# Order of the four token sums within each weight pass of the token-major projections

## The chip, the cores and the metric

The kernel runs on one core of a Trainium2 chip. The metric is device time in microseconds (us), the median over runs of one program. TensorE is called PE below, its weight loads PEld, VectorE DVE, ScalarE ACT, GpSimd POOL, and the queue that issues most transfers SP.

## What is computed

One layer of a diffusion backbone over 512 latent and 256 context tokens of width 1024, in float32. A combined projection of the modulated input feeds three branches (a gated linear recurrence, differential attention, a chunked spatial gate); each is gated, projected, scaled by a sigmoid gate and summed, and one output projection follows. What matters here is three of the products:

```
px = split_proj(modulate(x, sh_x, sc_x), w_in, b_in)      # px[6], px[7]: 512 tokens x 1024
sgu_x = spatial_gating(px[6], px[7], ln_g, ln_b, w_s, b_s)
...
return (s_a * y_a + s_b * y_b + s_c * y_c) @ w_out        # 512 tokens x 1024
```

`px[7]`, `px[6]` and the first 512 columns of the product with `w_out` are the three token-major projections of this document: the result has tokens on the partitions.

## The kernel before, in words

Every float32 operand is held as a high and a low part, and a product is three matmuls: high by high, high by low, low by high (`mm3`, lines 62 to 64). Most projections are channel-major: one weight tile of 128 columns, one PSUM sum of 512 tokens, 24 matmuls of 512 columns.

The token-major ones work on 512 output columns at a time. There are four sums, one for each block `tt` of 128 tokens; each is 128 x 512 float32. The four lie in two PSUM tiles of 128 x 1024 (`bk`, from the pool `big` of three): sums 0 and 1 share the first tile, 2 and 3 the second. A weight request of 512 rows (one half of the contraction) makes one pass: `proj_th` issues 12 matmuls for each `tt`, so a pass has 48. Two passes (`half` 0 and 1) complete the four sums. After the 12 matmuls of `half` 1 of a `tt`, DVE reads that sum out of PSUM: at line 1066 it adds the bias (`proj_tokens`, used for `vz`, sums named `sv`, and for `u`), at line 1225 it multiplies by the gate row (`residual`, sums named `out`), followed there by two more DVE operations (lines 1226 and 1228). `proj_tokens` does this for two column halves `j`, the output projection once. So five passes have readouts: those of the weights w61 and w63 (`sv`), w81 and w83 (`u`) and w109 (`out`). The passes of w60, w62, w80, w82 and w108 have none.

PE's instructions run in the order in which the program writes them. The other engines' order is made by the framework's scheduler. The framework keeps one record for each tile: a PE write to a tile waits for a readout of that tile that stands before it in the program, whichever columns either of them touches.

Weights come through three `raw` buffers of 512 KB (SP, lines 105 to 113), are cast on ACT (line 133) and their low part is formed on DVE or POOL (line 134). `pump` starts one such piece after each group of matmuls, once the weights that held the slot are used up.

```
for half in range(2):
    W = w_next()
    for tt in range(4):
        ps = bk[tt // 2][:, tt % 2 * 512:tt % 2 * 512 + 512]
        proj_th(ps, X, tt, W, half)
        pump()
        if half == 1:
            done = V.tensor_tensor(dst[:, tt, cs], ps, bias[:, cs], ALU.add)
```

Of the kernel before, what the change touches and what calls it, by code (L numbers as in the profile page):

```python
# [29 lines left out]
def block_kernel(ctx, tc, x, c, cctx_in, c_ctx, w_ada, b_ada, w_in, b_in, conv_w, conv_b,  # L30
# [19 lines left out]
    def big_t(name):  # L50
        return big.tile([P, 1024], F32, tag="big", name=name)
# [18 lines left out]
    def proj_th(ps, X, tt, W, half):  # L70
        mm3(ps, X, W, [np.s_[:, 4 * half + k, tt * P:(tt + 1) * P] for k in range(4)],
            [np.s_[:, k, :] for k in range(4)], half == 0, half == 1)
# [66 lines left out]
    def pump(n=1):  # L139
        for _ in range(n):  # L140
            if state["conv"] >= len(pieces):
                return
            i, part = pieces[state["conv"]]
            if part == 0 and not all(retired(x) for x in reqs[i][4]):
                return
            w_conv()

    def w_next():
        i = state["use"]
        state["use"] += 1  # L150
        while state["conv"] < len(pieces) and pieces[state["conv"]][0] <= i:
            w_conv()
        return parts[i]
# [900 lines left out]
    def proj_tokens(dst, bias, name, then=None):  # L1054

        for j in range(2):
            cs = slice(j * 512, j * 512 + 512)
            bk = [big_t(f"{name}{j}_{t}") for t in range(2)]
            for half in range(2):
                W = w_next()  # L1060
                for tt in range(4):
                    ps = bk[tt // 2][:, tt % 2 * 512:tt % 2 * 512 + 512]
                    proj_th(ps, X, tt, W, half)
                    pump()
                    if half == 1:
                        done = V.tensor_tensor(dst[:, tt, cs], ps, bias[:, cs], ALU.add)
                if then is not None:
                    then(2 * j + half, done if half else None)

    vz = sp.tile([P, 4, D], F32, name="vz")  # L1070
    def hs_a(step, done):
# [6 lines left out]
        with tc.issue_after(done.ins):  # L1078
            for g in range(8):
                V.tensor_tensor(hsA[:, 1, g, :], pa[:, g, :], f(hsA[:, 0, g, :]), ALU.subtract)  # L1080

    proj_tokens(vz, bvv, "sv", hs_a)
    lg = bcast(sgu_ln_g[0], "lg")
    lb = bcast(sgu_ln_b[0], "lb")
# [47 lines left out]

    u = gp.tile([P, 4, D], F32, tag="c", name="u")
    proj_tokens(u, bcast(b_in[0, 6 * D:7 * D], "bu"), "u")

    def sgu_mm(g):
# [85 lines left out]
    def residual(tt, c0, n, ps, j):  # L1222
        cs = slice(c0, c0 + n)
        tm = op.tile([P, 512], F32, tag="tm", bufs=2, name=f"tm{tt}_{j}")
        V.tensor_tensor(tm[:, 0:n], ps, gt[:, cs], ALU.mult)
        V.scalar_tensor_tensor(xr[:, tt, cs], xr[:, tt, cs], ALPHA, tm[:, 0:n], op0=ALU.mult,
                               op1=ALU.add)
        V.bn_stats(sto[:, tt, j, :], xr[:, tt, cs])
# [7 lines left out]
    bk = [big_t(f"out{t}") for t in range(2)]  # L1236
    for half in range(2):
        W = w_next()
        for tt in range(4):
            ps = bk[tt // 2][:, tt % 2 * 512:tt % 2 * 512 + 512]  # L1240
            proj_th(ps, M, tt, W, half)
            pump()
            if half == 1:
                residual(tt, 0, 512, ps, 0)
# [71 lines left out]
```

## Time and profile before

| what | value |
|---|---|
| median of 3 runs | 1033.73 us (1033.44 to 1035.08) |
| the profiled execution | 1034.09 us, of which its span is 1032.1 us |
| PE busy | 968.8 us (94%), 5239 matmuls |
| DVE busy | 659.7 us (64%) |
| ACT busy | 525.3 us (51%) |
| POOL busy | 155.0 us (15%) |
| mean granted clock of TensorE | 0.978 |
| transfers | 103.34 MB, mean 100 GB/s |

The span runs from the first to the last instruction. Busy time of PE is modelled: matmuls overlap, each lasting longer than the distance to the next. So the pace of PE is read from the starts of matmuls, not from their durations. A figure in brackets behind a row of a timeline is how long the engine was idle before it, and what ended the idle time.

### The profile page before, as it was taken

What the parts mean: (1) busy time and instruction counts of PE and PEld (TensorE: products, weight loads), DVE (VectorE), ACT (ScalarE), POOL (GpSimd) and SP (SyncE); (2) the same over time, 40 slices, a digit from 0 to 9 for tenths busy, and PEclk for the clock granted to TensorE, in tenths of its full rate; (3) what the DMA queues carried; (4) which work ended last, traced back from release to release, by engine and by line L of the source; (5) the groups of instructions that cost most, each with busy time, mean ns of one, the idle gap of its engine ahead of it and who ended that gap; (6) DMA issues with size and microseconds to landing.
All of it is one profiled execution on the core that took longest, in us unless ns stands there. A gap on an engine that the chain in (4) does not pass through costs nothing.

```text
span 1032.1 us, 13231 instructions
## 1 busy us (share of the span) xinstructions
PE 968.8 (94%) x5239; PEld 815.7 (79%) x5239; DVE 659.7 (64%) x996; ACT 525.3 (51%) x741; POOL 155.0 (15%) x118
## 2 busy tenths in 40 slices
PE   5997799989989998999999999899999999999996
PEld 4796688878878887778888887778887778888876
DVE  4479788788787663787777775368333256325557
ACT  3155846646647796897777795223221134323221
POOL 1143424333242252100000000000000000000002
PEclk8999999989989999899999999999999999999999
DMA  9933220130130131213332223625223322754212
GB/s 312 289 102 83 62 62 21 43 102 22 42 103 21 41 103 45 68 51 103 102 92 82 82 87 97 235 82 162 82 82 109 95 71 76 252 172 145 97 48 82
DMA packets 142996, 103.34 MB, mean 100 GB/s; under 512 B 3629, under 2 KB 133142, under 8 KB 142934
## 3 DMA queue, kind: packets, MB, share of 16 engines
q1 hardware_dynamic: 140790, 95.85, 30.4%
q0 software_dynamic: 2000, 6.56, 2.4%
q8 instruction: 41, 0.67, 0.3%
q14 instruction: 21, 0.17, 0.0%
q10 hardware_dynamic: 144, 0.10, 0.0%
HBM read 94.10 MB, written 4.19 MB: 95 GB/s over the span
## 4 chain that ended last, share of the span: by engine, by line
PE 64%; DVE 17%; ACT 11%; DMA 4%; issue 3%; SPq 1%; POOL 0%; POOLq 0%; ACTq 0%; DVEq 0%
PE y L62 4%; PE gt L62 4%; PE gt L64 4%; PE gt L63 4%; PE y L64 4%; PE y L63 4%; DVE mxn L732 2%; DVE e L747 2%; DVE kd L582 2%; ACT rt L859 1%; DVE kd L587 1%; PE s L722 1%; PE gc L62 1%; PE gc L64 1%; PE out L62 1%
## 5 line engine op out<-in xcount | busy, mean ns | idle before, releaser
L133 ACT CAST w<-raw 128x1024 fp32r<-128x1024 f32 x96 | 99.8, 1045 | 85.3 <-PE y L64 23.8
L134 DVE TENSOR_TENSOR w<-raw,w 128x1024 fp32r<-128x1024 f32 x71 | 86.6, 1224 | 77.5 <-ACT w L133 77.4
L62 PE MATMUL gt<-xhl,w 128*128 128x512 f32 x192 | 75.6, 394 | 1.3 <-ACT pad L882 1.3
L64 PE MATMUL gt<-xhl,w 128*128 128x512 f32 x192 | 74.8, 390 | 0.0
L63 PE MATMUL gt<-xhl,w 128*128 128x512 f32 x192 | 74.8, 390 | 0.0
L722 PE MATMUL s<-kd,qdq 128*128 128x512 f32 (+1 forms) x256 | 58.6, 368 | 17.2 <-ACT e L737 6.2
L134 POOL TENSOR_TENSOR w<-raw,w 128x1024 fp32r<-128x1024 f32 x25 | 61.0, 2444 | 67.5 <-ACT w L133 67.5
L722 PEld LDWEIGHTS s<-kd,qdq 128*128 128x128 f32 x256 | 44.4, 195 | 29.0 <-issue 15.0
L732 DVE TENSOR_REDUCE mxn<-s 128x1 f32<-128x768 f32 x64 | 58.3, 949 | 7.5 <-PE s L722 7.5
L737 ACT ACTIVATE e<-s,mxn 128x768 f32<-128x768 f32 x32 | 28.8, 899 | 51.1 <-DVE mxn L732 51.0
L1197 POOL PARTITION_BROADCAST grb<-grs x8 | 3.8, 581 | 308.3 <-DVE grs L1194 308.3
L62 PEld LDWEIGHTS gt<-xhl,w 128*128 128x128 f32 x192 | 36.1, 188 | 9.1 <-ACT pad L882 1.5
L64 PEld LDWEIGHTS gt<-xhl,w 128*128 128x128 f32 x192 | 36.0, 188 | 7.7
L63 PEld LDWEIGHTS gt<-xhl,w 128*128 128x128 f32 x192 | 36.1, 188 | 7.1
L964 POOL DMA_DIRECT2D pa_d<-ha x8 | 4.4, 551 | 227.4 <-DVE ha L963 227.4
L747 DVE SCALAR_TENSOR_TENSOR e<-s,sm,e 128x768 f32<-128x768 f32 x32 | 32.6, 1017 | 6.5 <-ACT e L740 5.7
L54 ACT CAST vh<-v 128x128 fp32r<-128x128 f32 x48 | 12.4, 263 | 43.0 <-PE v L64 19.7
L859 ACT ACT_TABLE_LOAD x25 | 32.1, 1283 | 0.4
L62 PE MATMUL xa<-xhl,w 128*128 128x512 f32 x64 | 26.3, 411 | 4.8 <-ACT pad L882 4.8
L765 DVE TENSOR_TENSOR wtl<-t,wth 128x768 fp32r<-128x768 f32 x32 | 30.3, 950 | 0.6 <-ACT wth L763 0.5
L740 ACT ACTIVATE e<-e,sm 128x768 f32<-128x768 f32 x32 | 29.9, 935 | 0.2 <-DVE sm L739 0.2
L859 ACT ACTIVATE rt<-ri,colB 128x770 f32<-128x770 f32 x32 | 27.6, 905 | 2.5 <-PE ri L64 1.8
(458 smaller groups left out, 3043.7 us busy)
## 6 DMA issues: line engine op xcount, KB each, us to landing
raw<-in_w_in_dram SPq DMA_DIRECT2D x96, 512.0 KB, 3.8
raw<-in_w_branch_dram SPq DMA_DIRECT2D x24, 512.0 KB, 3.9
ada<-in_w_ada_dram SPq DMA_DIRECT2D x6, 1024.0 KB, 8.4
qdq<-qdq POOLq DMA_DIRECT2D x16, 256.0 KB, 3.0
adg<-in_w_ada_dram SPq DMA_DIRECT2D x8, 512.0 KB, 6.0
raw<-in_w_out_dram SPq DMA_DIRECT2D x8, 512.0 KB, 3.8
xtok<-in_x_dram SPq DMA_DIRECT2D x4, 512.0 KB, 5.5
ada<-in_w_ada_dram SPq DMA_DIRECT2D x4, 512.0 KB, 6.0
```

What stands on the lines that cost most here:

```text
L62: PE.matmul(ps, ah, bh, start=(first and i == 0), stop=False)
L63: PE.matmul(ps, ah, bl, start=False, stop=False)
L64: PE.matmul(ps, al, bh, start=False, stop=(last and i == n - 1))
L133: state["hi"] = S.copy(h, raws[j])
L134: state["lo"].tensor_tensor(l, raws[j], f(h), ALU.subtract)
L722: PE.matmul(sp[:, sl], qds[h][:, 2 * m + j, qs], kds[h][:, m, sl], start=(j == 0), stop=(j == 1))
L732: V.tensor_reduce(mxn[:, m:m + 1], sps[m][:, 0:TA], mybir.AxisListType.X, ALU.max, negate=True)
L737: S.activation(e, sps[m][:, 0:TA], AF.Exp, bias=mxn[:, m:m + 1], accum_out=sm[:, m:m + 1])
L740: S.mul(es[i][0], es[i][0], sm[:, 0:1])
L747: V.scalar_tensor_tensor(e0, e1, sm[:, 1:2], e0, op0=ALU.mult, op1=ALU.add)
L765: V.tensor_tensor(wts[h][1][:, :, qs], src, f(wts[h][0][:, :, qs]), ALU.subtract)
L859: order[0] = S.activation(out, in_, fn, **kw)
```

## The change

In both places the loop over the four sums runs in the order 0, 2, 1, 3, for `half` 0 and `half` 1 alike.

```
@@ proj_tokens
             for half in range(2):
                 W = w_next()
-                for tt in range(4):
+                for tt in (0, 2, 1, 3):
                     ps = bk[tt // 2][:, tt % 2 * 512:tt % 2 * 512 + 512]
                     proj_th(ps, X, tt, W, half)
                     pump()
@@ the first 512 columns of the output projection
     for half in range(2):
         W = w_next()
-        for tt in range(4):
+        for tt in (0, 2, 1, 3):
             ps = bk[tt // 2][:, tt % 2 * 512:tt % 2 * 512 + 512]
             proj_th(ps, M, tt, W, half)
             pump()
```

First place, PE in the pass of w61: the three rows on either side of the border between the first and the second group of 12 matmuls, before. `sv_0` is the first PSUM tile (sums 0 and 1), `sv_1` the second; `waits DVE_49` is a wait for DVE's counter.

```order
L62 MATMUL sv_0_5596<-w61h,xhl 128x512
L63 MATMUL sv_0_5596<-w61l,xhl 128x512
L64 MATMUL sv_0_5596<-w61h,xhl 128x512
L62 MATMUL sv_0_5596<-w61h,xhl 128x512 [waits DVE_49]
L63 MATMUL sv_0_5596<-w61l,xhl 128x512
L64 MATMUL sv_0_5596<-w61h,xhl 128x512
```

The same engine and pass with the change, at the borders from the first group to the second and from the second to the third:

```order
L62 MATMUL sv_0_5596<-w61h,xhl 128x512
L63 MATMUL sv_0_5596<-w61l,xhl 128x512
L64 MATMUL sv_0_5596<-w61h,xhl 128x512
L62 MATMUL sv_1_5597<-w61h,xhl 128x512
L63 MATMUL sv_1_5597<-w61l,xhl 128x512
L64 MATMUL sv_1_5597<-w61h,xhl 128x512
...
L62 MATMUL sv_0_5596<-w61h,xhl 128x512 [waits DVE_49]
L63 MATMUL sv_0_5596<-w61l,xhl 128x512
L64 MATMUL sv_0_5596<-w61h,xhl 128x512
```

The second group now writes the other tile and has no wait; the wait on the first readout stands one group later, at the third. The wait at the fourth group, on the readout of the tile's first sum, stays at the fourth, but that sum is now the second group's and no longer the third's.

Second place, DVE in the same pass, from the low part of the next weights to the first row that follows the four readouts, before:

```order
L134 TENSOR_TENSOR w62l<-raw_0_5606,w62h 128x1024 [waits DMAHW4_49,Activation_49]
L134 TENSOR_TENSOR w62l<-raw_1_5624,w62h 128x1024 [waits DMAHW5_49,Activation_49]
L1066 TENSOR_TENSOR vz<-sv_0_5596,bvv 128x512 [waits DMAHW7_49,PE_49]
L1092 BN_STATS st_5874<-vz 128x6 [waits DVE_49]
L1066 TENSOR_TENSOR vz<-sv_0_5596,bvv 128x512 [waits PE_49]
L1092 BN_STATS st_5878<-vz 128x6 [waits DVE_49]
L1066 TENSOR_TENSOR vz<-sv_1_5597,bvv 128x512 [waits PE_49] x2
L1080 TENSOR_TENSOR hsA<-pa,hsA 128x512 [waits DMAHW0_49,Activation_49]
```

and with the change:

```order
L134 TENSOR_TENSOR w62l<-raw_0_5606,w62h 128x1024 [waits DMAHW4_49,Activation_49]
L134 TENSOR_TENSOR w62l<-raw_1_5624,w62h 128x1024 [waits DMAHW5_49,Activation_49]
L1066 TENSOR_TENSOR vz<-sv_0_5596,bvv 128x512 [waits DMAHW7_49,PE_49]
L1092 BN_STATS st_5874<-vz 128x6 [waits DVE_49]
L1066 TENSOR_TENSOR vz<-sv_1_5597,bvv 128x512 [waits PE_49]
L1066 TENSOR_TENSOR vz<-sv_0_5596,bvv 128x512 [waits PE_49]
L1092 BN_STATS st_5878<-vz 128x6 [waits DVE_49]
L1066 TENSOR_TENSOR vz<-sv_1_5597,bvv 128x512 [waits PE_49]
L1080 TENSOR_TENSOR hsA<-pa,hsA 128x512 [waits DMAHW0_49,Activation_49]
```

The readouts follow the new order of the sums; what stands ahead of the first readout (the next weights' low part) and behind the last has not moved. ACT, POOL and SP have the same rows in the same order as before.

## Rows read from the trace of the kernel before

**Rows 1.** The page, part 1: busy time, share of the span, instructions.

```profile
PE 968.8 (94%) x5239; PEld 815.7 (79%) x5239; DVE 659.7 (64%) x996; ACT 525.3 (51%) x741; POOL 155.0 (15%) x118
```

**Rows 2.** Waits of PE from 640 us to the end: total us, times, longest.

```profile
PE sv L62 <- DVE vz L1066: 4.2, 4, 1.5
PE u L62 <- DVE u L1066: 4.2, 4, 1.5
PE out L62 <- DVE tm L1225: 2.2, 2, 1.5
```

**Rows 3.** Timeline, pass of w61: start us, us, engine, line, operation.

```profile
656.47 0.39 PE L62 MATMUL sv<-w61h,xhl 128*128 128x512 f32 x1
...
660.08 0.68 DVE L1066 TENSOR_TENSOR vz<-sv,bvv 128x512 f32<-128x512 f32 x1
...
660.82 0.50 PE L62 MATMUL sv<-w61h,xhl 128*128 128x512 f32 x1 [1.47 <-DVE vz L1066]
...
663.88 0.69 DVE L1066 TENSOR_TENSOR vz<-sv,bvv 128x512 f32<-128x512 f32 x1 [2.38 <-PE sv L64]
...
666.17 0.39 PE L64 MATMUL sv<-w61h,xhl 128*128 128x512 f32 x1
...
667.35 0.50 PE L62 MATMUL sv<-w61h,xhl 128*128 128x512 f32 x1 [0.79 <-DVE vz L1066]
...
670.24 0.39 PE L62 MATMUL sv<-w62h,xhl 128*128 128x512 f32 x1
```

**Rows 4.** Timeline of PE: the first matmul of the other passes, or behind them.

```profile
681.12 0.39 PE L62 MATMUL sv<-w63h,xhl 128*128 128x512 f32 x1
...
694.63 0.39 PE L62 MATMUL gt<-xhl,w 128*128 128x512 f32 x1
...
793.75 0.39 PE L62 MATMUL u<-w81h,xhl 128*128 128x512 f32 x1
...
807.51 0.39 PE L62 MATMUL u<-w82h,xhl 128*128 128x512 f32 x1
...
818.39 0.39 PE L62 MATMUL u<-w83h,xhl 128*128 128x512 f32 x1
...
831.85 0.39 PE L62 MATMUL sgu<-vnh,wsh 128*128 128x512 f32 x1
...
986.89 0.39 PE L62 MATMUL out<-w109h,mhl 128*128 128x512 f32 x1
...
1000.63 0.28 PE L62 MATMUL out<-w110h,mhl 128*128 128x256 f32 x1
```

**Rows 5.** Timeline of DVE: first readouts of the other four passes, and w63's low part.

```profile
675.87 2.35 DVE L134 TENSOR_TENSOR w63l<-raw,w63h 128x1024 fp32r<-128x1024 f32 x2
...
684.46 0.68 DVE L1066 TENSOR_TENSOR vz<-sv,bvv 128x512 f32<-128x512 f32 x1
...
797.35 0.68 DVE L1066 TENSOR_TENSOR u<-u,bu 128x512 f32<-128x512 f32 x1
...
821.73 0.68 DVE L1066 TENSOR_TENSOR u<-u,bu 128x512 f32<-128x512 f32 x1
...
990.50 0.69 DVE L1225 TENSOR_TENSOR tm<-out,gt 128x512 f32<-128x512 f32 x1
```

**Rows 6.** Weight pieces (tile raw), 640 to 720 us: issue to landing.

```profile
DMA to landing us min/median/max: 3.4/4.2/5.0
```

**Rows 7.** Windows: stretch, length, busy us of each engine, granted clock (PEclk), DMA.

```profile
219.00:222.00 3.00, 3.00 (x16) 3.00 (x16) 3.00 (x5) 2.73 (x5) 2.64 (x2) 0.50 0.00 0
...
656.40:670.20 13.80, 11.55 (x50) 8.89 (x49) 5.74 (x7) 6.16 (x10) 0.06 (x1) 1.00 0.65 214
```

**Rows 8.** Timeline of PE where the granted clock is 0.50.

```profile
216.74 1.62 PE L722 MATMUL s<-kd,qdq 128*128 128x512 f32 x4 [1.87 <-DVE e L747]
...
218.15 0.41 PE L62 MATMUL v<-w15h,xhl 128*128 128x256 f32 x1
...
221.78 0.41 PE L64 MATMUL v<-w15h,xhl 128*128 128x256 f32 x1
```

More of the change, by code (lines that the diff above doesn't have):

```diff
@@ L1060, in proj_tokens @@
                 W = w_next()
-                for tt in range(4):
+                for tt in (0, 2, 1, 3):
                     ps = bk[tt // 2][:, tt % 2 * 512:tt % 2 * 512 + 512]
@@ L1238, in block_kernel @@
         W = w_next()
-        for tt in range(4):
+        for tt in (0, 2, 1, 3):
             ps = bk[tt // 2][:, tt % 2 * 512:tt % 2 * 512 + 512]
```

## The prediction

> **What bounds the kernel now.** I read the shares of the engines first: PE is busy 94% of the span, the next engine 64% [rows 1]. So the time is PE's own work plus its gaps, and a change that adds no matmul can only act through gaps. The list of PE's waits, from 640 us to the end, comes next: apart from one wait for a weight in the pass of w60, the only waits there are ten, always of a first matmul (line 62) for a readout by DVE: four in `sv`, four in `u`, two in `out` [rows 2]. The channel-major projections between them, some 230 us, show none. The timeline of one pass with readouts then shows how such a wait comes about [rows 3]. The first group of 12 matmuls runs from 656.47; at the pace found below its last starts at 656.47 + 11 x 0.2267 = 658.96, and the next matmul, which belongs to sum 1 in the same tile, starts only at 660.82, right behind the readout of sum 0 (660.08 to 660.76). The third group, in the other tile, starts without a wait while sum 1 is read out (663.88). Then sum 3 waits for the readout of sum 2: 666.17 to 667.35. The reader is to see that each tile costs one wait, and that a readout under matmuls of the other tile holds nobody up: it lasts 0.69 us there, against 0.68 us with PE idle.
>
> **The change part by part.**
>
> *The pace without a wait.* The pass of w62, with no readouts, starts at 670.24 [rows 3] and ends at 681.12 [rows 4]: 10.88 us for 48 matmuls, 0.2267 us each. The pass of w82, 807.51 to 818.39, takes 10.88 us too [rows 4]. Each changes the sum three times and the tile once within those 10.88 us, so changing the target costs nothing that these rows show.
>
> *What a pass with readouts loses now.* Its length less 10.88 us: w61, 656.47 to 670.24, 13.77 us, so 2.89 [rows 3]; w63, 681.12 to 694.63, 13.51, so 2.63; w81, 793.75 to 807.51, 13.76, so 2.88; w83, 818.39 to 831.85, 13.46, so 2.58; w109, 986.89 to 1000.63, 13.74, so 2.86 [rows 4]. The sum is **13.84 us**. In w61 the waits themselves, from start to start less one step, are 1.86 - 0.23 = 1.63 us and 1.18 - 0.23 = 0.95 us [rows 3]; the other 0.3 us of a pass are the slower starts just behind a wait (a matmul of 0.50 us instead of 0.39). I take the length of the passes, since it holds both.
>
> *What the moved waits cost.* With the change the third group waits for the first readout. It is due at pass start + 24 x 0.2267 = 5.44 us. In the pass of w61 that is 661.91; the readout, which stands behind the low part of w62 on DVE and so does not begin when the first group ends, finished at 660.76 [rows 3]: 1.15 us to spare. In the others, with the ends of the first readouts [rows 5] against pass start + 5.44 [rows 4]: w63, 685.14 against 686.56, 1.42 to spare; w81, 798.03 against 799.19, 1.16; w83, 822.41 against 823.83, 1.42; w109, 991.19 against 992.33, 1.14. What comes ahead of these readouts hangs on the end of the pass before, so it keeps its distance from the pass. The fourth group waits for the readout of sum 2. That sum's last matmul ends about 5.6 us into the pass; The first readout ends 4.0 to 4.3 us into the pass by the figures above; what DVE has behind it is at most two operations on 512 columns (`out`) or some statistics (`sv`, lines 1092 and 1093), so it is free by about 6 us, the readout takes 0.7, and the group is due at 8.16 us: over a microsecond to spare. So the ten waits go to zero. Nothing in these rows prices a satisfied wait at a group's start on PE. From below it is nothing: each of the passes without readouts begins with a matmul that waits for a cast long done, and 0.2267 us is kept. From above it is what a matmul behind a wait loses, 0.50 - 0.39 = 0.11 us, ten times 1.1 us. I take nothing, since the nearer rows are those of the passes without readouts, and keep 1.1 us for the range.
>
> *What is hidden.* DVE's four readouts of a pass are the same instructions in another order; they lie under PE. With the third group's sum read later than before, the next tile taken from the pool follows a readout that ends about 9 us into the pass, and its first write comes in the second group of the next pass, at 10.88 + 2.72 = 13.60 us: some 4.6 us to spare. In the output projection two more operations on the same 512 columns follow each readout; counted as long as it (0.69 us [rows 5]), they make 2.1 us for a group of 12 x 0.2267 = 2.72 us of PE, and fit.
>
> *What follows earlier.* Casts and low parts of the next weights start when a pass ends, so they move up with PE. The shortest distance I find is w63's low part: done at 675.87 + 2.35 = 678.22 [rows 5], first used at about 681.35, 3.1 us later; both ends move up by w61's 2.89. Only transfers keep their own length, 3.4 to 5.0 us from issue to landing [rows 6], issued a pass or more ahead. The tail behind PE's last matmul does not change.
>
> *The sum.* The profiled execution took 1034.09 us; less 13.84 is 1020.25. The median of the runs lies 0.36 us below the profiled one, so the forecast for a median is 1033.73 - 13.84 = **1019.9 us**.
>
> *Rule against row.* The rows say that a group which goes on in the same 1024-wide tile waits 1.63 and 0.95 us [rows 3]. The Trainium skill (Perfetto Trace Analysis, Matmuls) says that independent groups should rotate through PSUM banks so that the readout of one overlaps the matmuls of the next, and (PSUM — Partial Sum Buffer, Terms and Specifications) that a bank holds 512 float32 values of a partition. By that rule alone the kernel before rotates already, one bank for each sum, the readouts are covered, and the change gains 0: 1033.7. The rows disagree with this reading: what counts in this program is the tile, and the tile holds two banks.
>
> **The rivals.**
>
> *A readout comes late.* If DVE reaches a first readout more than some 1.2 us later than now (it has a low part ahead of it, 2.35 us long where w63's stands [rows 5]), the third group waits. At worst the five first waits come back in full: 1.63 us in w61, w81 and w109, and 0.26 less in w63 and w83, whose passes lose that much less: 3 x 1.63 + 2 x 1.37 = 7.6 us, and the time is about 1027.5. Against it: the low part hangs on a cast that starts at a fixed point of the pass. For it: the reserve is smallest, 1.14 us, in three of the five.
>
> *The gain is given back behind.* PE gets 13.84 us ahead of the transfers. If a weight piece now lands late by its spread of 5.0 - 3.4 = 1.6 us [rows 6] at two points, some 3.2 us come back: about 1023. Against it: PE waits for no weight behind 656 us today.
>
> *It does nothing.* The wait could follow the second group wherever it is, if the record were coarser than a tile: 1033.7. Against it: sum 2 starts without a wait while sum 1 is read [rows 3]. By the Trainium skill's rule above the result would be the same.
>
> *Slower: the granted clock.* With PE at 0.50 (its 1.2 GHz level) 18 matmuls of 256 columns start 0.2135 us apart (218.15 to 221.78, 17 steps [rows 7, 8]), so 512 columns would take 0.427, 0.20 more than now; a pass would take 9.6 us longer. If the new rhythm of tiles lowered the clock in two passes, they would cost 19.2 us against the 13.84 gained: about 1039. It decides from 13.84 / 0.20 = 69 matmuls on, a pass and a half. Against it: the clock is 1.00 in a pass with both waits in it [rows 7], PE gets busier, and where the clock is 0.50, PE came out of a wait of 1.87 us for the softmax [rows 8], longer than any that this change leaves. The Trainium skill (TensorE: Matmul & The Clock Gate, A second HAM failure mode: psum-queue depth-cycling) tells of a kernel whose cycling through PSUM banks made PE idle briefly between groups, so that the clock swung; by that rule the alternation would cost. The trace has three changes of sum in each pass at 1.00, so it does not bear this out here.
>
> **How the numbers follow.** Forecast 0.87; late readouts 0.05; given back behind 0.04; nothing 0.03; slower clock 0.01. A measurement can tell about 0.2%, 2 us, from no change. The forecast and the first two rivals are faster by far more: 0.96. Nothing is the 0.03 of same, the clock the 0.01 of slower. The range: the runs lie from 0.3 us below to 1.35 us above their median, so the forecast alone gives 1019.6 to 1021.3; 1.1 us for satisfied waits makes that 1022.4; up to about 1023.4 it takes in the weights' late landing. Below I add 1 us, since the runs spread over 1.64 us and three others can have their median elsewhere in that. So 1018.6 to 1023.4.
>
> **What would show it.** Right: the passes of w61, w63, w81, w83 and w109 last about 10.9 us each; the ten waits are gone from PE's list and nothing takes their place; DVE's readouts last 0.7 us still; the clock stays 1.00. Wrong: a wait of a third group for line 1066 or 1225 (late readouts), a wait for line 133 or 134 behind 656 us (given back), or matmuls of 512 columns 0.43 us apart (the clock).

## The result

| | median us | lowest to highest | runs |
|---|---|---|---|
| before | 1034.24 | 1033.44 to 1035.08 | 4 |
| with the change | 1019.13 | 1019.10 to 1021.12 | 4 |

The ratio is 0.9859, with a 95% interval of 0.9842 to 0.9876. The forecast, 1019.9 against 1033.73, was a ratio of 0.9866.

The page of the changed kernel, its span and part 1 (it answers to [rows 1]):

```profile
span 1017.1 us, 13232 instructions
...
PE 965.0 (95%) x5239; PEld 816.1 (80%) x5239; DVE 659.4 (65%) x996; ACT 525.5 (52%) x741; POOL 154.9 (15%) x118
```

The same 5239 matmuls, in a span that is 15.0 us shorter. The list of what PE waited for from 640 us to the end (it answers to [rows 2]; the columns are total us, times, longest):

```profile
PE sv L63 <- DVE w60l L134: 1.1, 1, 1.1
```

The ten waits for readouts are gone and none has come in their place. The one that is left, for the low part of w60, was there before. The timeline of the pass of w61 (it answers to [rows 3]):

```profile
655.39 0.39 PE L62 MATMUL sv<-w61h,xhl 128*128 128x512 f32 x1
...
656.72 2.36 DVE L134 TENSOR_TENSOR w62l<-raw,w62h 128x1024 fp32r<-128x1024 f32 x2 [10.23 <-ACT w62h L133]
...
657.89 0.39 PE L64 MATMUL sv<-w61h,xhl 128*128 128x512 f32 x1
...
658.11 0.39 PE L62 MATMUL sv<-w61h,xhl 128*128 128x512 f32 x1
...
659.00 0.69 DVE L1066 TENSOR_TENSOR vz<-sv,bvv 128x512 f32<-128x512 f32 x1
...
660.83 0.39 PE L62 MATMUL sv<-w61h,xhl 128*128 128x512 f32 x1
...
661.03 0.69 DVE L1066 TENSOR_TENSOR vz<-sv,bvv 128x512 f32<-128x512 f32 x1 [0.62 <-PE sv L64]
...
663.55 0.39 PE L62 MATMUL sv<-w61h,xhl 128*128 128x512 f32 x1
...
666.27 0.39 PE L62 MATMUL sv<-w62h,xhl 128*128 128x512 f32 x1
```

The second group starts 0.22 us after the last matmul of the first, while sum 0 has not been read out yet: DVE is at the low part of w62 until 659.08. The third group, which needs that readout, is due at 660.83; the readout ended at 659.69. The fourth, at 663.55, needs the readout that ended at 661.72. The pass takes 666.27 - 655.39 = 10.88 us.

The other passes with readouts, by the first matmul of each and the one that follows it (they answer to [rows 4]):

```profile
677.15 0.39 PE L62 MATMUL sv<-w63h,xhl 128*128 128x512 f32 x1
...
688.03 0.39 PE L62 MATMUL gt<-xhl,w 128*128 128x512 f32 x1
...
787.17 0.39 PE L62 MATMUL u<-w81h,xhl 128*128 128x512 f32 x1
...
798.05 0.39 PE L62 MATMUL u<-w82h,xhl 128*128 128x512 f32 x1
...
808.93 0.39 PE L62 MATMUL u<-w83h,xhl 128*128 128x512 f32 x1
...
819.81 0.39 PE L62 MATMUL sgu<-vnh,wsh 128*128 128x512 f32 x1
...
974.82 0.39 PE L62 MATMUL out<-w109h,mhl 128*128 128x512 f32 x1
...
985.70 0.28 PE L62 MATMUL out<-w110h,mhl 128*128 128x256 f32 x1
```

All four take 10.88 us, like that of w61, and to the hundredth what a pass without readouts takes. Two of them as windows of the profile (length, busy us of each engine, then the granted clock):

```profile
655.40:666.30 10.90, 10.90 (x50) 9.03 (x49) 5.74 (x7) 6.16 (x10) 0.00 (x0) 1.00 0.84 273
...
974.80:985.70 10.90, 10.90 (x49) 9.01 (x48) 8.40 (x11) 2.00 (x2) 0.00 (x0) 1.00 0.16 50
```

PE has no idle time in either, and the clock is 1.00, the upper of its two levels, as it was [rows 7].

**Where the 14.94 us come from.** The two profiled executions took 1034.09 and 1019.15 us. The first matmul of w60's pass, ahead of all that the change touches, started here before the change and with it:

```profile
643.73 0.39 PE L62 MATMUL sv<-w60h,xhl 128*128 128x512 f32 x1
```

```profile
642.62 0.39 PE L62 MATMUL sv<-w60h,xhl 128*128 128x512 f32 x1
```

So 1.11 us of the difference arose earlier, in code that has not changed. From there to the end of the execution it is 1034.09 - 643.73 = 390.36 us before and 1019.15 - 642.62 = 376.53 with the change: **13.83 us**, where the sum of the prediction had 13.84. This figure, from w60's first matmul to the end, is used for all experiments below, since what comes ahead of it differs from run to run by more than the terms in question. It is not free of noise itself: it holds the 1.8 to 2.0 us by which the time of an execution exceeds its span. So a second figure stands beside it, which lies inside the span: from w60's first matmul to the first of w110, the weights behind the five passes. It is 1000.63 - 643.73 = 356.90 us before and 985.70 - 642.62 = 343.08 with the change, 13.82 us less.

### The profile page after: what moved, and what is told of

It is laid out like the page before. It is cut to its first block, busy times and chain, and to the rows that moved or that the text cites. A ratio compares the mean times of both kernels' runs of the same rounds, so it can differ in the third digit from the quotient of the medians.

```text
span 1017.1 us, 13232 instructions
## 1 busy us (share of the span) xinstructions
PE 965.0 (95%) x5239; PEld 816.1 (80%) x5239; DVE 659.4 (65%) x996; ACT 525.5 (52%) x741; POOL 154.9 (15%) x118
## 4 chain that ended last, share of the span: by engine, by line
PE 68%; DVE 16%; ACT 10%; issue 3%; DMA 2%; SPq 0%; POOL 0%; POOLq 0%; ACTq 0%; DVEq 0%
PE y L62 4%; PE gt L62 4%; PE gt L64 4%; PE gt L63 4%; PE y L64 4%; PE y L63 4%; DVE mxn L732 2%; DVE e L747 2%; DVE kd L582 2%; ACT rt L859 1%; PE out L63 1%; PE out L64 1%; PE out L62 1%; PE s L722 1%; PE gc L62 1%
```

## The experiments

Times are medians in us; each kernel's runs were taken beside runs of the kernel before, whose median there was 1034.34 for own_tiles, order_0231, proj_only and read_x4, and 1033.27 for the other four. The last two columns are as above, from the profiled execution. Edits are shown against the changed kernel, that of own_tiles against the kernel before.

| kernel | median | ratio to before, interval | from w60 | w60 to w110 |
|---|---|---|---|---|
| before | 1034.24 | | 390.36 | 356.90 |
| the change | 1019.13 | 0.9842 to 0.9876 | 376.53 | 343.08 |
| own_tiles | 1020.70 | 0.9850 to 0.9885 | 376.34 | 343.07 |
| order_0231 | 1025.35 | 0.9904 to 0.9933 | 381.89 | 348.58 |
| proj_only | 1023.23 | 0.9881 to 0.9911 | 379.42 | 345.94 |
| out_only | 1031.17 | 0.9967 to 0.9986 | 387.77 | 354.30 |
| half1_only | 1019.56 | 0.9846 to 0.9890 | 376.37 | 343.08 |
| read_x2 | 1019.57 | 0.9846 to 0.9886 | 376.32 | 343.08 |
| read_x4 | 1025.24 | 0.9902 to 0.9932 | 381.87 | 348.42 |
| swap_slots | 1017.97 | 0.9829 to 0.9864 | 374.64 | 341.20 |

**Is it the shared tile, or the order?** `own_tiles` keeps the old order and gives each sum a tile.

```
-            bk = [big_t(f"{name}{j}_{t}") for t in range(2)]
+            bk = [(big_t, acc_t)[t % 2](f"{name}{j}_{t}") for t in range(4)]
             ...
                 for tt in range(4):
-                    ps = bk[tt // 2][:, tt % 2 * 512:tt % 2 * 512 + 512]
+                    ps = bk[tt][:, 0:512]
```

(and the same in the output projection)

> Order 0, 1, 2, 3 as before, but each of the four sums has a PSUM tile of its own (two from the pool big, two from acc), so neighbours in time share none. Theory (the wait is one for each tile that is written again behind a readout): the ten waits of PE for lines 1066 and 1225 are gone, each pass with readouts takes 10.9 us, the time is within 1 us of the changed kernel, 1019 to 1020 us. Rival (the order or its rhythm matters, not the sharing; or DVE reads too late in any case): PE still waits in the second and fourth groups, passes of 13.5 to 13.8 us, about 1034 us.

Measured: 376.34 us from w60; PE's only wait from 640 us on is for the low part of w60; all five passes take 10.88 us, that of w61 from 659.02 to 669.90:

```profile
PE sv L63 <- DVE w60l L134: 1.1, 1, 1.1
```

```profile
659.02 0.39 PE L62 MATMUL sv<-w61h,xhl 128*128 128x512 f32 x1
...
669.90 0.39 PE L62 MATMUL sv<-w62h,xhl 128*128 128x512 f32 x1
```

The order 0, 1, 2, 3 costs nothing once no neighbours share a tile. In the kernel before, sums 0 and 1 lay in different columns too, 0 to 511 and 512 to 1023, and yet PE waited: what counts is the tile. The median of `own_tiles` lies 1.6 us above that of the change, but its profiled execution was already 3.65 us behind at w60's first matmul (646.27 against 642.62), ahead of the first of these tiles; from there to w110 it takes 343.07 us, the change 343.08.

**One neighbour in place of two.** `order_0231` lets the second and third groups share a tile.

```
-                for tt in (0, 2, 1, 3):
+                for tt in (0, 2, 3, 1):
```

(in both places)

> Order 0, 2, 3, 1: the second and third groups share a tile, the first and second do not, nor the third and fourth. Theory: one wait is left in each pass with readouts, of the kind that the second tile had before (0.95 us and 0.15 us of slow starts behind it), at the third group. Five passes of about 12.0 us, 5 x 1.1 = 5.5 us more than the changed kernel, about 1024.7 us. Rival (what counts is the PSUM bank, or only the wait behind the first readout): no wait, 1019 us. Rival (any neighbours in one tile bring back both waits): 1034 us.

Measured: 381.89 - 376.53 = 5.36 us more than the change, or 5.50 from w60 to w110, where 5.5 was expected. The five passes take 12.00, 11.96, 12.00, 11.97 and 11.98 us. PE's waits in `sv`, `u` and `out`:

```profile
PE u L62 <- DVE u L1066: 1.6, 2, 0.8
PE sv L62 <- DVE vz L1066: 1.6, 2, 0.8
...
PE out L62 <- DVE tm L1225: 0.8, 1, 0.8
```

and the one in the pass of w61, with the readout that it follows:

```profile
661.11 0.69 DVE L1066 TENSOR_TENSOR vz<-sv,bvv 128x512 f32<-128x512 f32 x1 [0.62 <-PE sv L64]
...
661.86 0.50 PE L62 MATMUL sv<-w61h,xhl 128*128 128x512 f32 x1 [0.78 <-DVE vz L1066]
```

Five waits in place of ten, each of the shorter kind, each right behind the readout of the group just ahead. So it is not the bank alone that counts (sums 2 and 3 lie in different halves of their tile, which the prediction counts as two banks), nor only the first readout, and one pair of neighbours brings back one wait.

**The parts add up.** `proj_only` has the new order in `proj_tokens` alone, `out_only` in the output projection alone.

```
@@ proj_only: the output projection
-        for tt in (0, 2, 1, 3):
+        for tt in range(4):
@@ out_only: proj_tokens
-                for tt in (0, 2, 1, 3):
+                for tt in range(4):
```

> The new order in the two token-major projections of the input (sv, u), the old one in the output projection. Theory: the passes of w61, w63, w81 and w83 take 10.9 us, that of w109 13.7 us with its two waits for line 1225; 2.86 us more than the changed kernel, about 1022.0 us. Rival (part of the gain is given back behind sv and u and only the output projection's lasts): more than 1025 us.

Measured: 379.42, 2.89 us more than the change (2.86 from w60 to w110), with the two waits of `out` (2.2 us) as before and w109's pass at 13.75 us.

> The new order in the output projection alone, the old one in sv and u. Theory: the pass of w109 takes 10.9 us, the four others 13.5 to 13.8; 2.86 us less than before, about 1031.3 us, and 387.5 us from the first matmul of w60's pass to the end (390.4 before). Rival (DVE, busiest near the end, gives it back in the last projections): nothing, 1034 us and 390 us.

Measured: 387.77, so 2.59 us less than before; w109's pass takes 10.88 us. Its gain shows in the runs too (0.9967 to 0.9986). It falls 0.27 short of 2.86, and 0.22 of that is w63's pass, which with the old order took 13.73 us in this execution where it had taken 13.51: the low part ahead of its first readout began 1.30 us into the pass here and 1.06 there, so PE's first wait was longer by about as much (1.44 us in the row, against 1.20). The two parts give 390.36 - 379.42 = 10.94 and 2.59 us, 13.53 together, or 13.75 with that pass set equal. DVE gave nothing back in the last projections: it is busiest there (before, 23.94 of 31.37 us, against 167.48 of the 356.90 from w60 to w110), but from w110's first matmul to the end the executions took 33.46 us before and 33.47 here.

**Only the passes with readouts.** `half1_only` keeps the old order in `half` 0.

```
-                for tt in (0, 2, 1, 3):
+                for tt in ((0, 1, 2, 3), (0, 2, 1, 3))[half]:
```

(in both places)

> The new order in the passes with readouts (half 1) alone; half 0 keeps 0, 1, 2, 3. Theory: the passes without readouts had no waits to lose, so nothing differs from the changed kernel: from the first matmul of w60's pass to the end of the execution 376.5 us as there, and about 1019 to 1020 us. Rival (the order of half 0 matters too, through the tiles' first writes): waits in the passes of w60, w62, w80, w82 or w108, more than 377 us from w60's start.

Measured: 376.37; the passes with readouts take 10.88 us and the one wait of PE from 640 us on is that for w60. The order of `half` 0 makes no difference here.

**How much room the third group has.** `read_x2` and `read_x4` repeat the readout of sum 0 in `sv` and `u`, once and three times more.

```
                     if half == 1:
+                        if tt == 0:
+                            for _ in range(1):   # read_x4: range(3)
+                                V.tensor_tensor(dst[:, tt, cs], ps, bias[:, cs], ALU.add)
                         done = V.tensor_tensor(dst[:, tt, cs], ps, bias[:, cs], ALU.add)
```

> The changed kernel, with the readout of sum 0 in sv and u done twice, which ends it some 0.7 us later. Theory: the 1.15 to 1.42 us to spare hold it; no wait at the third groups, 376.5 us from w60's first matmul to the end, 1019 to 1020 us. Rival (each readout's delay shows in full): 4 x 0.7 = 2.8 us more.

Measured: 376.32, no wait, every pass at 10.88 us. The 0.7 us fit into the room.

> The changed kernel, with the readout of sum 0 in sv and u done four times over (the same result each time), which ends it some 3 x 0.72 = 2.2 us later. Theory (the third group waits for that readout and had 1.15 us to spare in w61 and w81, 1.42 us in w63 and w83): PE waits in the third groups of these four passes, about 1.0, 0.75, 1.0 and 0.75 us, with 0.15 us of slow starts each 4.1 us in all, about 1023.2 us; the pass of w109 stays at 10.9 us. Rival (the third group does not hang on the first readout, or has far more room): no wait, 1019 us.

Measured: 381.87, 5.34 us more than the change instead of 4.1 (5.34 from w60 to w110 too). The passes of w61, w63, w81 and w83 took 12.56, 11.87, 12.57 and 11.86 us, that of w109 10.88. DVE in the pass of w61 of this kernel, whose readouts are lines 1068 (the repeats) and 1069:

```profile
659.17 2.13 DVE L1068 TENSOR_TENSOR vz<-sv,bvv 128x512 f32<-128x512 f32 x3
661.22 1.28 DVE L1069 TENSOR_TENSOR vz<-sv,bvv 128x512 f32<-128x512 f32 x2
```

and the third group there and in w63's pass, in the latter with the pair of readouts in which it starts:

```profile
662.55 0.50 PE L62 MATMUL sv<-w61h,xhl 128*128 128x512 f32 x1 [1.39 <-DVE vz L1069]
...
684.51 1.29 DVE L1069 TENSOR_TENSOR vz<-sv,bvv 128x512 f32<-128x512 f32 x2
...
685.26 0.50 PE L62 MATMUL sv<-w63h,xhl 128*128 128x512 f32 x1 [0.65 <-DVE vz L1069]
```

The pair at line 1069 is the fourth readout of sum 0 and the readout of sum 2. The view does not name the sums; the times tell their order. In w61 the third group starts at 662.55, 0.05 us after the pair ended, so the fourth readout of sum 0 was the second of the two; in w81 it is the same (796.98 against 796.93). In w63 the group starts inside the pair (684.51 to 685.80), so there that readout was the first; w83 is like it. So in w61 and w81 the readout of sum 2 stood in the way, which the expectation had not counted. Against the expected losses of 1.15 and 0.9 us, w61 and w81 lost 1.68 and 1.69 us, some 0.5 more each, and w63 and w83 0.99 and 0.98, some 0.1 more: 1.2 us in all, and 4.1 + 1.2 = 5.3. The room itself, 1.15 and 1.42 us, is bracketed by the two kernels: 0.7 us are hidden, 2.2 us are not.

**The wait that is left.** PE's list with the change has one entry from 640 us on, for the low part of w60. The weights of w61, needed one pass later, stand ready before it: their low part is done at 640.00, while the first piece of w60's begins only when the matmuls of `ga`, the last before w60's pass, have ended, and PE waits for it until 644.16.

```profile
638.77 1.23 DVE L134 TENSOR_TENSOR w61l<-raw,w61h 128x1024 fp32r<-128x1024 f32 x1 [0.62 <-ACT w61h L133]
...
642.88 1.23 DVE L134 TENSOR_TENSOR w60l<-raw,w60h 128x1024 fp32r<-128x1024 f32 x1 [2.88 <-PE ga L64]
```

```profile
644.16 0.50 PE L63 MATMUL sv<-w60l,xhl 128*128 128x512 f32 x1 [1.15 <-DVE w60l L134]
```

If the reason is that w61's slots come free earlier, exchanging the two pairs of slots takes the wait away. `swap_slots` does that.

```
     for n in range(2):
-        want(f"t{n}", src, c0, (2 * n, 2 * n + 1))
+        want(f"t{n}", src, c0, (2 - 2 * n, 3 - 2 * n))
```

> The changed kernel, with the two pairs of weight slots exchanged in every token-major pair of requests, so that w60's weights go to the slots that come free first. In the changed kernel PE waits for w60's low part, and w60's pass takes 12.8 us where 10.9 would do, while w61's stands ready. Theory: w60's pass takes 10.9 us, 1.9 us off the changed kernel from w60's first matmul to the end (376.5 to 374.6), about 1017.3 us. Rival: the wait moves to w61's low part or to the cast ahead of the branch's last sums, and nothing is gained.

Measured: 374.64 from w60, 1.89 us less than the change, and w60's pass takes 10.88 us instead of 12.77. DVE makes w60's low part while PE is still at the branch sums, and w61's in time for the next pass:

```profile
633.75 2.36 DVE L134 TENSOR_TENSOR w60l<-raw,w60h 128x1024 fp32r<-128x1024 f32 x2
...
644.00 1.23 DVE L134 TENSOR_TENSOR w61l<-raw,w61h 128x1024 fp32r<-128x1024 f32 x1 [4.73 <-PE ga L64]
...
645.81 1.22 DVE L134 TENSOR_TENSOR w61l<-raw,w61h 128x1024 fp32r<-128x1024 f32 x1
```

w61's pass starts at 654.63, more than 7 us after that, and PE's list of waits is empty from 640 us to the end. Its median, 1017.97, is the lowest of all kernels here, but its interval overlaps that of the change, and in the whole time 1.9 us are within what runs differ by; that it gains is shown by the pass, and by the 341.20 us to w110 against 343.08.

## Why the prediction was right

- **The bound.** PE's gaps were the only thing to gain, and of them the ten waits for readouts. Right: with them gone PE has no idle time in the five passes, and the instructions of each engine are as many as before. The eleventh wait, for w60's weight, which the prediction named and left, was worth another 1.89 us (`swap_slots`).
- **The pace and the loss of each pass.** The sum of 13.84 us was taken from the lengths of the passes, not from the waits in the list (4.2 + 4.2 + 2.2 = 10.6 us [rows 2]). Measured were 13.83. That the two agree to a hundredth says little of the last digits: sum and measurement start from the same execution of the kernel before, and in another one with the old order (`out_only`) w63's pass took 13.73 us instead of 13.51. The list alone would have missed 3.2 us: the time it counts begins at the modelled end of a matmul, 0.39 us after its start, where the next would have started after 0.23, and the slower starts behind a wait are not in it. `order_0231` shows the same: 4.0 us of waits in its list, 5.5 us of time.
- **The moved waits.** Taken as zero, with 1.1 us kept for the range. Right: 10.88 us in every pass leaves nothing for ten satisfied waits. The room of the third group in w61 was put at 1.15 us; it is 660.83 - 659.69 = 1.14 us in the changed kernel, and `read_x2` and `read_x4` lie on either side of it. One reading failed without effect: what comes ahead of a first readout was to keep its distance from the pass. In w63 it did not. The low part there began 1.06 us into the pass before and 1.34 with the change, so the readout ended at 681.45 where the third group was due at 682.59: 1.14 us of room, where 1.42 was forecast.

```profile
680.77 0.68 DVE L1066 TENSOR_TENSOR vz<-sv,bvv 128x512 f32<-128x512 f32 x1
```

- **What follows earlier.** Right: no wait for a weight appeared behind the passes. The shortest distance that the prediction named was kept: w63's low part was done at 674.25, 2.90 us ahead of its pass at 677.15, and before at 678.22, 2.90 ahead of 681.12.
- **Rule against row.** The Trainium skill (Perfetto Trace Analysis, Matmuls) asks that independent groups rotate through PSUM banks. By that rule the kernel before needed nothing. The rows were followed, and `own_tiles` and `order_0231` confirm them: the unit to rotate through is the tile by which this program waits. With each sum in its own tile the readouts overlap the matmuls of the next group, and the passes take 10.88 us.
- **The rivals.** No readout came late, nothing was given back, and the clock stayed at 1.00 in the passes. `read_x4` made the first rival happen: the waits come back in the third group, as it said, once the room is used up.
- **What the sum did not hold.** The time came out 0.8 us below the forecast, and the medians differ by 15.11 us, 1.3 more than the passes give. So the nearness of the number owes something to luck. The profiled executions differ by 1.11 us ahead of w60's pass, in code that is the same, and no step of the prediction speaks of it; the range covered it with the spread of the runs.

## What to carry to other kernels

When PE waits for a readout in the middle of a stretch of matmuls, look at which tile the next group writes, not only which columns of it: under a framework that keeps its record by tile, as here, a group waits for the readout of its neighbour in the same tile. Either give each its own tile or order them so that neighbours in time lie in different tiles; one group in between was 2.72 us of cover here, of which 1.58 us had gone in w61 when the readout ended, 0.97 of them on the rest of a low part ahead of it, and then 0.69 on the readout itself; with that readout done four times the cover was too short. And price such a wait from the lengths of the stretch with and without it, because the waits listed are less than the time that they cost.

## What was not expected of the hardware

What comes ahead of w60's pass differs from execution to execution by more than most of the terms above. Among the profiled executions of these kernels w60's first matmul started between 641.91 and 646.27 us, while from there to w110's the change, `own_tiles`, `half1_only` and `read_x2` agree to 0.01 us. Some of it arises in the first tenth: the first matmul of line 722 started between 90.19 and 93.49 us. Some arises later: from there to w60's first matmul it took 551.92 to 552.78 us in nine of the ten executions and 549.63 in `read_x2`, which was not looked into. In `own_tiles`, the latest, 3.21 of the 3.65 us behind the change were there at line 722 (93.49 against 90.28), and PE's waits in the first 90 us hold

```profile
PE v L62 <- DVE vl L55: 5.1, 1, 5.1
PE ada L334 <- DMA ada<-in_w_ada_dram: 2.9, 3, 1.7
```

and in the changed kernel

```profile
PE v L62 <- DVE vl L55: 4.1, 1, 4.1
...
PE ada L334 <- DMA ada<-in_w_ada_dram: 1.2, 2, 0.9
```

Together 2.7 us lie in these two. Why they differ, in code that is the same, was not tried.
